# Seven block products for eight: folding 14 units in each of the second and the third feed-forward network, with ten modulation rows moved from the one to the other

## The chip, the cores and the metric

The kernel runs on one core of a Trainium2 chip, as one program. The metric is the device time of one execution in microseconds (us). Engines are named as in the profile: PE is TensorE (matmuls), DVE is VectorE, ACT is ScalarE, SP is SyncE, which here issues the loads.

## The reference

A two-layer transformer with 256 latent tokens (LAT) and 256 context tokens (CTX), width 1024, in fp32. Each layer has a mixer (attention in the first, an mLSTM in the second) between two half feed-forward networks (FFN). The change touches the FFN and the modulation:

```python
def half_ffn(h, shift, scale, gate, w_in, w_out, g, b):
    xm = modulate(h, shift, scale)              # h * (1 + scale) + shift
    a, u = jnp.split(xm @ w_in, 2, axis=-1)     # hidden width D_FF = 2816
    y = (jax.nn.silu(a) * u) @ w_out
    return post_norm(h, 0.5 * gate * y, g, b)   # layer norm of ALPHA * h + delta
```

Shift, scale and gate come from nine 1024-wide modulation vectors per layer, each a 1024 x 1024 block of a matrix times the silu of the conditioning. There is one conditioning vector for LAT and one for CTX.

## The kernel before

**Products.** Activations lie as 8 tiles of 128 features by 512 tokens (LAT in columns 0 to 255, CTX in 256 to 511). Every fp32 value is held as a high and a low fp32r part, so that each product is three matmuls: high-high, high-low and low-high (`mm3`). A loaded fp32 weight chunk of 128x1024 is split in `split`: ScalarE makes the high part (L207), VectorE the low one (L212). Chunks come over the SP queue in program order into raw buffers (4) and are split into pair buffers (7).

**FFN.** There are four, numbered li = 2 * layer + s; "second FFN" is li 1 and "third FFN" is li 2. The hidden width is 22 units of 128. A unit is 48 matmuls with 512 columns (16 products) and gives two PSUM tiles, a and u. ScalarE and VectorE make silu(a) * u from them (L534, L535) and split the result (L212) into the pair `gt[j]`. The units come in parts (11 and 11, or 6, 8 and 8). After the units of a part follow its out products: for each of 8 output tiles d, one product for each unit of the part, and VectorE adds the sum to the residual (L582). The first four units of an FFN (the lead) run on LAT first and then on CTX, with 256 columns, so that they can start while CTX of the stage before is still being normed. In the same way the last d's of the last part (the tail: 4 of them, 6 in the third FFN) run on LAT first and then on CTX. The layer norm of LAT begins inside the LAT tail, after the product that the tables `TAILSTEP` and `FOLDSTEP` name: step m is its sums over features on TensorE (L393), and L486 to L488 write the normed tiles, while TensorE goes on with the rest of LAT and with CTX.

**Folded units.** In the third FFN the units of the second and the third part (16 of 22) are computed with seven block products of half size in place of eight, by Strassen's scheme. A unit is then 84 matmuls of 256 columns (L718) instead of 48 of 512. It needs sums of weight blocks on VectorE (`fold_w`: four sums L689 to L692 of 512 elements, and splits; the first product uses the block "11" that was loaded, the second the sum "s2", which is ready last but one). Sums of activation blocks are made once per FFN (`fold_x`, two calls within the out products of the first part).

**Modulation rows.** A row is one 128x1024 tile of `ada_w`, loaded by `ada_load` (L297) into one of two buffers, and multiplied by the conditioning in `ada_dot` (L303), one dot of 1024 elements on VectorE for each conditioning vector: "both" rows have two dots, single rows one. Rows stand in a list for each FFN and are popped at written-out places: after units ("in"), after out products ("out"). Where a list is used up, a pop does nothing. VectorE carries out its instructions in the program's order, so a dot whose row hasn't landed holds up all that stands behind it.

Of the kernel before, what the change touches and what calls it, by code (L numbers as in the profile page):

```python
# [24 lines left out]
CTX = (256, 512)  # L25
BOTH = (0, 512)
NF = 22
NFH = 11
# [8 lines left out]
RMS_EPS = 1e-6  # L37
HEADS = 8
MH = 4
FOLD = {2: (6, 8, 8)}  # L40
FOLDTAIL = 6
FOLDPOP = {
    2: {
        "lead": (2, 2, 2, 2),
        "in": {4: 3, 5: 3},
        "out": {0: (0, 0, 0, 0, 1, 1, 1, 1), 1: (2, 2, 2, 2, 2, 2, 1, 1)},
    },
}
FOLDX = {0: 0, 2: 1}
# [105 lines left out]
class Body:  # L155
# [382 lines left out]
    def ffn(self, layer, s, gate, groups, side, start=None):  # L538
        nc, V = self.nc, self.nc.vector
        li = layer * 2 + s  # L540
        allg = BOTH
        call = lambda *k: side.get(k, lambda: None)()
        fold = li in FOLD
        parts = FOLD.get(li, (NFH, NFH))
        tail, tailstep = (FOLDTAIL, FOLDSTEP) if fold else (TAIL, TAILSTEP)
        ends = np.cumsum(parts).tolist()
        with self.tc.tile_pool(name=f"ffn{li}", bufs=1) as gp:
# [40 lines left out]
            for hf in range(len(parts)):  # L588
# [12 lines left out]
                        call("in", j)  # L601
                    js = js[LEAD:]
                folded = None
                if fold and hf:
                    self.fine = False
                    folded = self.folded(js, w_in)
                    js = []
# [25 lines left out]
                for d in range(begun, body):  # L633
                    unit_out(hf, d, w, allg)
                    call("out", hf, d)
                    if fold and not hf and d in FOLDX:
                        self.fold_x(2 * FOLDX[d])
                if body < ND:
                    w = Keep(self, w.chunks, SH, w)
                    self.fine = True  # L640
                    for g in groups:
                        for d in range(body, ND):
                            unit_out(hf, d, w, g, tailstep)
                    self.steps(ENDSTEP)


# [783 lines left out]
def emit(ctx, tc, a, out):  # L1430
    b = Body(ctx, tc, a, out)
    nc, V, S = b.nc, b.nc.vector, b.nc.scalar
    b.setup()
    b.setup_rest()
    cpool = b.silu_c()
    both2 = (0, 1)
    queue = [
        [(0, p, both2) for p in range(16, 72)],
        [(1, p, both2) for p in range(40)],
        [(1, p, (0,)) for p in range(40, 72)],  # L1440
    ]
    made = {}

    def once(key, f):
        def get():
            if key not in made:
                made[key] = f()
            return made[key]
        return get

    def side(key, coef, keep=(True, True), nxt=True, ada=(), alone=False, fold=None):
        def pop(n=None):
            for _ in range(n if n is not None else 3 if len(ada) > 40 else 2):
                if ada:
                    b.ada(*ada.pop(0))

        get = once(key, coef)

        b.begin = lambda g: b.norm(g, get, keep[0 if g == LAT else 1], nxt, alone)
        s = {}  # L1460
        if fold:
            for j, n in enumerate(fold["lead"]):
                s["in", j] = lambda n=n: pop(n)
            for j, n in fold["in"].items():
                s["in", j] = lambda n=n: pop(n)
            for hf, ns in fold["out"].items():
                for d, n in enumerate(ns):
                    s["out", hf, d] = lambda n=n: pop(n)
            return s
        for j in range(NF):  # L1470
            s["in", j] = pop
        for d in range(ND):
            s["out", 0, d] = pop
        return s

    both = (LAT, CTX)
    b.ffn(0, 0, once("g0", lambda: b.half_gate(0, 2)), both, side("n0", lambda: b.ln_mod(0, 0, (0, 3)), ada=queue[0]), start)
    assert not queue[0]
    cpool.close()
    b.attention(lambda: b.shift_(0, 5), side("n1", lambda: b.ln_mod(0, 1, (0, 6))))  # L1480
    cpool = b.silu_c()
    b.silu_load()
    b.ffn(0, 1, once("g1", lambda: b.half_gate(0, 8)), both, side("n2", lambda: b.ln_mod(0, 2, (1, 0)), ada=queue[1]))
    assert not queue[1]
    b.ffn(1, 0, once("g2", lambda: b.half_gate(1, 2)), both, side("n3", lambda: b.ln_mod(1, 0, (1, 3)), (True, False), ada=queue[2], fold=FOLDPOP[2]))
    assert not queue[2]
    cpool.close()
    b.mlstm(lambda: b.shift_(1, 5, slice(0, 1)), side("n4", lambda: b.ln_mod(1, 1, (1, 6), 1), alone=True))
    b.ffn_last(1, once("g3", lambda: b.half_gate(1, 8, 1)))
# [5 lines left out]
def _layout(inputs):  # L1495
# [8 lines left out]
    A["ada_w"] = f("ada_w").transpose(0, 2, 1).reshape(2, 72, P, D)  # L1504
    w = f("ffn_w_in").reshape(4, ND, P, 2, NF, P).transpose(0, 4, 2, 1, 3, 5)
    w_in = w.reshape(4, NF, P, 2, 1024).transpose(0, 1, 3, 2, 4).reshape(4, 2 * NF, P, 1024).copy()
    for li, parts in FOLD.items():
        for j in range(parts[0], NF):
            u = w[li, j, :, :, 1, :]
            w_in[li, 2 * j] = w[li, j, :, :, 0, :].reshape(P, 1024)  # L1510
            w_in[li, 2 * j + 1] = np.concatenate([u[:, ND // 2 :], u[:, : ND // 2]], axis=1).reshape(P, 1024)
# [1 line left out]
    A["start_in"] = w[0, :NSTART].transpose(2, 1, 0, 3, 4).reshape(ND, P, 1024)  # L1513
    w = f("ffn_w_out").reshape(4, 2, NFH, P, ND, P).transpose(0, 1, 4, 2, 3, 5)
    w = w.reshape(4, NF * ND, P, P)
    for li, parts in FOLD.items():
        v, at = f("ffn_w_out").reshape(4, NF, P, ND, P)[li].transpose(0, 2, 1, 3), 0
        blocks = []
        for n in parts:
# [69 lines left out]
```

## Time and profile before

| | us |
|---|---|
| median of 3 runs | 1684.46 (1683.39 to 1686.16) |
| the profiled execution, its own time | 1681.06 |
| its span in the trace | 1679.2 |
| mean granted TensorE clock | 0.993 |
| TensorE (PE) busy | 1627.0 (97%) |
| VectorE (DVE) busy | 1328.8 (79%) |
| ScalarE (ACT) busy | 701.3 (42%) |

The profiled execution lies 3.4 us below the median. Times of single places are from the trace, in us from the start of the span. In it the second FFN runs from 578.8 to 948 and the third from 948 to 1304.

### The profile page before, as it was taken

To read this page: it belongs to the slowest core of one execution; us is meant where nothing else is said; L and a number is where in the kernel's file an instruction comes from. 1 tells how busy PE (TensorE), PEld (TensorE's weight loads), DVE (VectorE), ACT (ScalarE), POOL (GpSimd) and SP (SyncE) were. 2 spreads that over 40 slices of the span, in tenths; PEclk is the share of its full clock that TensorE was granted. 3 is DMA by queue.
4 is the path that set the end of the run, shared out by engine and by line. 5 is a ranking of instruction groups with operands and counts; after the bars stand their busy time and mean duration, and the time that the engine had idled before them with its cause. 6 is when DMAs were issued, how large, how long until landed. Compare 5 with 4: busy or idle time off the path is not lost.

```text
span 1679.2 us, 26198 instructions
## 1 busy us (share of the span) xinstructions
PE 1627.0 (97%) x10020; PEld 1454.3 (87%) x10020; DVE 1328.8 (79%) x2864; ACT 701.3 (42%) x1230; POOL 93.4 (6%) x114
## 2 busy tenths in 40 slices
PE   7999999999899999999999999899999999999997
PEld 6888888899888998888888998898999888999986
DVE  6799977749988889996334899887886967997686
ACT  5622222315566362322231452452462656566541
POOL 0000000002321100000000100000001002120000
PEclk9999999999999999999999999999999999999999
DMA  9577766522202337775232254446342332337552
GB/s 355 202 227 232 241 209 194 175 63 86 63 1 68 110 115 226 238 243 170 92 96 89 94 191 144 137 137 193 123 151 76 108 126 76 116 124 250 178 176 74
DMA packets 71918, 250.58 MB, mean 149 GB/s; under 512 B 7921, under 2 KB 10481, under 8 KB 71793
## 3 DMA queue, kind: packets, MB, share of 16 engines
q1 hardware_dynamic: 71072, 248.15, 45.4%
q8 instruction: 78, 1.28, 0.3%
q10 hardware_dynamic: 720, 0.76, 0.1%
q14 instruction: 48, 0.39, 0.1%
HBM read 247.83 MB, written 1.05 MB: 148 GB/s over the span
## 4 chain that ended last, share of the span: by engine, by line
PE 74%; DVE 17%; DMA 4%; ACT 3%; issue 2%; POOL 0%; ACTq 0%; DVEq 0%; SPq 0%; POOLq 0%
PE t L224 19%; PE t L228 19%; PE t L227 19%; DVE t L212 5%; PE t L718 4%; PE t L836 4%; PE t L1333 2%; ACT t L207 2%; DMA t<-in_ada_w 1%; DMA t<-in_ffn_in 1%; PE t L894 1%; PE t L896 1%; PE t L895 1%; PE t L393 1%; DVE t L486 1%
## 5 line engine op out<-in xcount | busy, mean ns | idle before, releaser
L224 PE MATMUL t<-t,t 128*128 128x512 f32 (+2 forms) x2288 | 758.5, 333 | 10.0 <-ACT t L207 6.7
L227 PE MATMUL t<-t,t 128*128 128x256 f32 (+2 forms) x2288 | 759.6, 333 | 1.5 <-DVE t L488 1.2
L228 PE MATMUL t<-t,t 128*128 128x256 f32 (+2 forms) x2288 | 756.2, 332 | 2.5 <-DVE t L212 2.5
L207 ACT CAST t<-t 128x1024 fp32r<-128x1024 f32 (+2 forms) x501 | 426.1, 873 | 534.7 <-PE t L228 231.8
L212 DVE TENSOR_TENSOR t<-t,t 128x256 fp32r<-128x256 f32 (+2 forms) x846 | 528.0, 660 | 137.2 <-ACT t L207 134.7
L224 PEld LDWEIGHTS t<-t,t 128*128 128x128 f32 x2288 | 429.8, 189 | 55.3 <-ACT t L207 9.1
L228 PEld LDWEIGHTS t<-t,t 128*128 128x128 f32 x2288 | 430.5, 188 | 45.9 <-DVE t L212 3.4
L227 PEld LDWEIGHTS t<-t,t 128*128 128x128 f32 x2288 | 431.2, 189 | 45.1 <-DVE t L488 2.1
L303 DVE SCALAR_TENSOR_TENSOR t<-t,t 128x1024 bf16<-128x1024 f32 x224 | 263.0, 1220 | 12.6 <-DMA t<-in_ada_w 12.5
L718 PE MATMUL t<-t,t 128*128 128x256 f32 x1344 | 159.5, 281 | 6.6 <-ACT t L207 4.2
L718 PEld LDWEIGHTS t<-t,t 128*128 128x128 f32 x1344 | 158.0, 191 | 8.4 <-ACT t L207 4.4
L534 ACT ACTIVATE t<-t 128x512 f32<-128x512 f32 (+1 forms) x77 | 37.9, 498 | 148.0 <-PE t L228 147.1
L535 DVE TENSOR_TENSOR t<-t,t 128x512 f32<-128x512 f32 (+1 forms) x77 | 42.9, 562 | 69.4 <-PE t L228 60.8
L430 POOL TENSOR_TENSOR t<-t,t 128x256 f32<-128x256 f32 x30 | 23.3, 777 | 1153.3 <-ACT t L420 1151.8
L582 DVE SCALAR_TENSOR_TENSOR t<-t,t,t 128x256 f32<-128x256 f32 x112 | 50.1, 478 | 40.4 <-PE t L228 40.1
L894 PE MATMUL t<-t,t 128*128 128x256 f32 (+1 forms) x256 | 79.1, 311 | 0.0
L896 PE MATMUL t<-t,t 128*128 128x256 f32 (+1 forms) x256 | 78.6, 309 | 0.0
L895 PE MATMUL t<-t,t 128*128 128x256 f32 (+1 forms) x256 | 78.4, 308 | 0.0
L1333 PE MATMUL t<-t,t 128*128 128x512 f32 (+1 forms) x248 | 55.3, 376 | 10.4 <-ACT t L287 4.9
L1333 PEld LDWEIGHTS t<-t,t 128*128 128x128 f32 x248 | 46.7, 222 | 18.6 <-ACT t L287 4.9
L836 PE MATMUL t<-t,t 128*128 128x512 f32 x264 | 60.0, 389 | 0.0
L836 PEld LDWEIGHTS t<-t,t 128*128 128x128 f32 x264 | 49.5, 188 | 10.2
(185 smaller groups left out, 1250.3 us busy)
## 6 DMA issues: line engine op xcount, KB each, us to landing
t<-in_ffn_in SPq DMA_DIRECT2D x168, 512.0 KB, 4.2
t<-in_ada_w SPq DMA_DIRECT2D x139, 512.0 KB, 4.0
t<-in_ffn_out SPq DMA_DIRECT2D x66, 512.0 KB, 4.2
t<-in_ffn_last SPq DMA_DIRECT2D x22, 512.0 KB, 3.5
t<-in_att_in SPq DMA_DIRECT2D x12, 512.0 KB, 3.5
t<-in_att_out SPq DMA_DIRECT2D x8, 512.0 KB, 3.9
t<-in_ml_qk SPq DMA_DIRECT2D x8, 512.0 KB, 3.4
t<-in_ml_v SPq DMA_DIRECT2D x8, 512.0 KB, 4.4
```

Source lines behind the costliest of these rows:

```text
L207: self.behind(self.nc.scalar.copy(h, x))
L212: self.behind(self.nc.vector.tensor_tensor(out=ls, in0=xs, in1=hs.bitcast(F32), op=ALU.subtract))
L224: ins = mm(out, wh, xh, start=first, stop=False)
L227: mm(out, wh, xl, start=False, stop=False)
L228: mm(out, wl, xh, start=False, stop=last)
L303: ins = nc.vector.scalar_tensor_tensor(self.tmp().bitcast(BF16), r, 1.0, self.cb[:, v, :], ALU.mult, ALU.mult, accum_out=to)
L718: self.pin(nc.tensor.matmul(o, p, q, start=first and k == i == 0, stop=k == half - 1 and i == 2, skip_group_check=True))
L836: pin(nc.tensor.matmul(ys[tt][i], gs[g], ws[k][w][:, i * 512 : (i + 1) * 512], start=k == 0 and g == w == 0, stop=k == NF - 1 and g == 1,))
L894: mm(o, self.xh[:, k, c], wh, start=k == 0, stop=False)
L895: mm(o, self.xh[:, k, c], wl, start=False, stop=False)
L896: mm(o, self.xl[:, k, c], wh, start=False, stop=k == ND - 1)
L1333: mm = lambda *k, **kw: pin(nc.tensor.matmul(*k, **kw))
```

## The change

The second FFN gets three parts of 8, 7 and 7 units instead of 11 and 11, and its last two parts are folded. The third goes from 6, 8 and 8 to 8, 7 and 7. So the number of folded units goes from 0 to 14 in the second and from 16 to 14 in the third. Ten both-rows move from the second FFN's list (40 to 30 rows) to the third's (32 single rows to 10 both and 32 single), and the pops get new tables. The tail of the second FFN has 6 d's instead of 4. Line numbers after the change are 5 or 6 higher than those of before.

```diff
-FOLD = {2: (6, 8, 8)}
+FOLD = {1: ((8, 7, 7), 1), 2: ((8, 7, 7), 1)}
 FOLDTAIL = 6
 FOLDPOP = {
+    1: {
+        "in": {0: 1, 1: 1, 2: 2, 3: 2, 4: 3, 5: 3, 6: 2, 7: 2},
+        "out": {0: (0, 0, 0, 0, 1, 1, 1, 1), 1: (1, 1, 1, 1, 1, 1, 0, 0), 2: (1, 1)},
+        "tail": {(0, 2): 1, (0, 3): 1},
+    },
     2: {
-        "lead": (2, 2, 2, 2),
-        "in": {4: 3, 5: 3},
-        "out": {0: (0, 0, 0, 0, 1, 1, 1, 1), 1: (2, 2, 2, 2, 2, 2, 1, 1)},
+        "in": {0: 3, 1: 3, 2: 3, 3: 3, 4: 5, 5: 5, 6: 4, 7: 4},
+        "out": {0: (0, 0, 0, 0, 1, 1, 1, 1), 1: (2, 2, 2, 2, 2, 2, 0, 0)},
+        "tail": {},
     },
 }
...
-        parts = FOLD.get(li, (NFH, NFH))
+        parts, folds = FOLD.get(li, ((NFH, NFH), 2))
...
-                if fold and hf:
+                if hf >= folds:
                     self.fine = False
                     folded = self.folded(js, w_in)
                     js = []
...
-                    if fold and not hf and d in FOLDX:
+                    if fold and hf == folds - 1 and d in FOLDX:
                         self.fold_x(2 * FOLDX[d])
...
                             unit_out(hf, d, w, g, tailstep)
+                            call("tail", int(g == CTX), d - body)
...
-        [(1, p, both2) for p in range(40)],
-        [(1, p, (0,)) for p in range(40, 72)],
+        [(1, p, both2) for p in range(30)],
+        [(1, p, both2) for p in range(30, 40)] + [(1, p, (0,)) for p in range(40, 72)],
```

The two dots of a both-row stand at three places of the third FFN's order where there were fewer before.

First place: VectorE in the third FFN, the CTX half of the lead, between the product of unit 0 (L535, after the change L540) and that of unit 1. L303 (L308) are dots, L212 (L217) splits of weights. Before:

```order
L535 TENSOR_TENSOR t_9112<-t_9112,t_9063 128x256
L212 TENSOR_TENSOR t_9319<-t_9317,t_9319 128x256
L212 TENSOR_TENSOR t_8801<-t_9112,t_8800 128x256
L303 SCALAR_TENSOR_TENSOR t_9120,t_9117<-t_9118,t_5623 128x1024
L303 SCALAR_TENSOR_TENSOR t_9124,t_9117<-t_9122,t_5623 128x1024
L212 TENSOR_TENSOR t_9319<-t_9317,t_9319 128x256 x3
```

And now:

```order
L217 TENSOR_TENSOR t_9560<-t_9871,t_9559 128x256
L308 SCALAR_TENSOR_TENSOR t_9878,t_7955<-t_9876,t_5623 128x1024
L308 SCALAR_TENSOR_TENSOR t_9880,t_7955<-t_9876,t_5623 128x1024
L308 SCALAR_TENSOR_TENSOR t_9884,t_7955<-t_9882,t_5623 128x1024
L308 SCALAR_TENSOR_TENSOR t_9886,t_7955<-t_9882,t_5623 128x1024
L217 TENSOR_TENSOR t_10115<-t_10113,t_10115 128x256 x3
L217 TENSOR_TENSOR t_10147<-t_10145,t_10147 128x256
L308 SCALAR_TENSOR_TENSOR t_9891,t_9888<-t_9889,t_5623 128x1024
```

Two dots of two rows have become six dots of three rows (the sixth stands behind the piece shown).

Second place: VectorE before the third FFN's out products of the first part. t_9473 is the product of the last plain unit before the change (unit 5), t_10374 and t_10461 are those of units 6 and 7 after it. Before:

```order
L303 SCALAR_TENSOR_TENSOR t_9399,t_9388<-t_9397,t_5623 128x1024
L212 TENSOR_TENSOR t_9752<-t_9750,t_9752 128x256 x2
L535 TENSOR_TENSOR t_9473<-t_9473,t_9406 128x512
L212 TENSOR_TENSOR t_9800<-t_9796,t_9800 128x1024
L212 TENSOR_TENSOR t_9472<-t_9473,t_9471 128x512
```

And now:

```order
L308 SCALAR_TENSOR_TENSOR t_10292,t_10285<-t_10290,t_5623 128x1024
L308 SCALAR_TENSOR_TENSOR t_10296,t_10285<-t_10294,t_5623 128x1024
L308 SCALAR_TENSOR_TENSOR t_10300,t_10285<-t_10298,t_5623 128x1024
L540 TENSOR_TENSOR t_10374<-t_10374,t_10307 128x512
L217 TENSOR_TENSOR t_10373<-t_10374,t_10372 128x512
L308 SCALAR_TENSOR_TENSOR t_10381,t_10285<-t_10379,t_5623 128x1024
L308 SCALAR_TENSOR_TENSOR t_10385,t_10285<-t_10383,t_5623 128x1024
L308 SCALAR_TENSOR_TENSOR t_10389,t_10285<-t_10387,t_5623 128x1024
L308 SCALAR_TENSOR_TENSOR t_10393,t_10285<-t_10391,t_5623 128x1024
L540 TENSOR_TENSOR t_10461<-t_10461,t_10400 128x512
```

The products of units 6 and 7 stand behind five and four dots, each of a row of its own.

Third place: TensorE in those out products after the change (L229, L232, L233 are the three matmuls of `mm3`; t_10372 and t_10373 are the high and low part of `gt[6]`, t_10459 and t_10460 those of `gt[7]`; t_10503 to t_10676 are the PSUM tiles of d 0 to 4):

```order
L229 MATMUL t_10644<-t_10372,t_10647 128x512
L232 MATMUL t_10644<-t_10373,t_10647 128x512
L233 MATMUL t_10644<-t_10372,t_10647 128x512
L229 MATMUL t_10503<-t_10459,t_10506 128x512
L229 MATMUL t_10560<-t_10459,t_10563 128x512
L229 MATMUL t_10592<-t_10459,t_10595 128x512
L232 MATMUL t_10503<-t_10460,t_10506 128x512
L233 MATMUL t_10503<-t_10459,t_10506 128x512
```

The products of the four first d's with units 0 to 6 stand ahead of the first one with unit 7. That is 84 matmuls of the out products, and the first one with unit 6 has 42 of them ahead of it.

Fourth place: VectorE at the end of the third FFN's first out products. L587 (before L582) is the sum of a d, L695 to L698 (L689 to L692) are the sums of weight blocks of the first folded units. Before:

```order
L582 SCALAR_TENSOR_TENSOR t_66<-t_9737,t_9545,t_66 128x256 x2
L690 TENSOR_TENSOR t_9798<-t_9798,t_9796 128x512
L303 SCALAR_TENSOR_TENSOR t_9769,t_9766<-t_9767,t_5623 128x1024
L582 SCALAR_TENSOR_TENSOR t_66<-t_9771,t_9545,t_66 128x256 x2
L303 SCALAR_TENSOR_TENSOR t_9794,t_9766<-t_9792,t_5623 128x1024
L691 TENSOR_TENSOR t_9796<-t_9796,t_9798 128x512
```

And now:

```order
L587 SCALAR_TENSOR_TENSOR t_66<-t_10748,t_10533,t_66 128x256 x2
L217 TENSOR_TENSOR t_10787<-t_10785,t_10787 128x1024
L308 SCALAR_TENSOR_TENSOR t_10782,t_10466<-t_10780,t_5623 128x1024
L217 TENSOR_TENSOR t_10824<-t_10820,t_10824 128x1024
L217 TENSOR_TENSOR t_10827<-t_10822,t_10827 128x512
L695 TENSOR_TENSOR t_10822<-t_10822 128x512
L696 TENSOR_TENSOR t_10822<-t_10822,t_10820 128x512
```

The split of the out products' last weight chunk (t_10787, for d 7) and the splits of the first folded unit's blocks stand here now, behind the sums of d 6. Before the change those splits stood ahead of the sums.

## Rows read from the trace of the kernel before

**Rows 1.** The page's busy times, shares and counts of each engine.

```profile
PE 1627.0 (97%) x10020; PEld 1454.3 (87%) x10020; DVE 1328.8 (79%) x2864; ACT 701.3 (42%) x1230; POOL 93.4 (6%) x114
```

**Rows 2.** Windows, all engines: start:end, length, busy us (instructions), granted clock, DMA share, GB/s.

```profile
628.20:913.80 285.60, 285.60 (x1262) 236.49 (x1261) 191.36 (x309) 76.41 (x91) 0.00 (x0) 1.00 0.53 169
980.70:1057.60 76.90, 72.25 (x392) 62.37 (x391) 68.57 (x143) 25.66 (x38) 0.00 (x0) 0.99 0.56 192
1183.40:1238.20 54.80, 54.70 (x479) 54.51 (x480) 47.03 (x72) 29.88 (x54) 0.00 (x0) 1.00 0.31 97
```

**Rows 3.** Windows of L718 alone (the folded units' matmuls), both blocks.

```profile
1050.50:1134.10 83.60, 78.47 (x648) 77.75 (x648) 0.96 0.43 136
1180.50:1256.40 75.90, 74.31 (x648) 73.72 (x648) 1.00 0.40 125
```

**Rows 4.** Timeline, first folded unit of the third FFN: start, duration, [idle before].

```profile
1050.58 1.58 PE L718 MATMUL t<-t,t 128*128 128x256 f32 x12
1052.15 1.23 DVE L303 SCALAR_TENSOR_TENSOR t<-t,t 128x1024 bf16<-128x1024 f32 x1 [0.50 <-DMA t<-in_ada_w]
1053.91 0.69 DVE L689 TENSOR_TENSOR t<-t 128x512 f32<-128x512 f32 x1
1054.51 0.69 DVE L692 TENSOR_TENSOR t<-t 128x512 f32<-128x512 f32 x1
1056.38 0.79 PE L718 MATMUL t<-t,t 128*128 128x256 f32 x2 [4.22 <-ACT t L207]
1057.64 1.43 PE L718 MATMUL t<-t,t 128*128 128x256 f32 x5 [0.47 <-DVE t L212]
```

**Rows 5.** Windows, all engines, behind that wait (columns as in rows 2).

```profile
1056.40:1063.00 6.60, 6.13 (x27) 5.84 (x28) 4.84 (x5) 2.38 (x4) 0.00 (x0) 0.50 0.52 169
1063.00:1066.00 3.00, 3.00 (x27) 3.00 (x27) 1.83 (x2) 3.00 (x5) 0.00 (x0) 1.00 0.00 1
```

**Rows 6.** VectorE's groups by form: count, busy us, mean ns, idle before.

```profile
L303 DVE SCALAR_TENSOR_TENSOR t<-t,t 128x1024 bf16<-128x1024 f32 x224 | 263.0, 1220 | 12.6 <-DMA t<-in_ada_w 12.5
L212 DVE TENSOR_TENSOR t<-t,t 128x512 fp32r<-128x512 f32 x120 | 81.3, 684 | 11.9 <-ACT t L207 11.6
L582 DVE SCALAR_TENSOR_TENSOR t<-t,t,t 128x256 f32<-128x256 f32 x112 | 50.1, 478 | 40.4 <-PE t L228 40.1
```

**Rows 7.** Timeline of VectorE behind the second FFN's lead.

```profile
632.15 1.22 DVE L303 SCALAR_TENSOR_TENSOR t<-t,t 128x1024 bf16<-128x1024 f32 x1
633.29 0.08 DVE L303 DVE_READ_ACCUMULATOR t<-t,t 128x1 f32 x1
...
635.59 1.22 DVE L212 TENSOR_TENSOR t<-t,t 128x1024 fp32r<-128x1024 f32 x1
637.54 1.23 DVE L303 SCALAR_TENSOR_TENSOR t<-t,t 128x1024 bf16<-128x1024 f32 x1 [0.74 <-DMA t<-in_ada_w]
...
640.16 1.23 DVE L303 SCALAR_TENSOR_TENSOR t<-t,t 128x1024 bf16<-128x1024 f32 x1 [0.24 <-DMA t<-in_ada_w]
```

**Rows 8.** Timeline of VectorE at the third FFN's last lead unit.

```profile
996.81 0.08 DVE L303 DVE_READ_ACCUMULATOR t<-t,t 128x1 f32 x1
...
1003.84 1.23 DVE L303 SCALAR_TENSOR_TENSOR t<-t,t 128x1024 bf16<-128x1024 f32 x1 [1.78 <-DMA t<-in_ada_w]
```

**Rows 9.** Windows of the dots (L303) alone: third FFN, second FFN.

```profile
980.70:1057.60 76.90, 21.84 (x36) 0.99 0.56 192
629.00:742.00 113.00, 70.21 (x120) 1.00 0.74 234
```

**Rows 10.** Timeline, the second FFN's tail and the LAT norm inside it.

```profile
926.70 0.70 PE L393 MATMUL t<-t,t 128*128 128x256 f32 x2
...
948.46 1.28 DVE L488 SCALAR_TENSOR_TENSOR t<-t,t,t 128x256 fp32r<-128x256 f32 x3
...
948.72 0.28 PE L227 MATMUL t<-t,t 128*128 128x256 f32 x1
948.84 0.28 PE L228 MATMUL t<-t,t 128*128 128x256 f32 x1
```

More of the change, by code (lines that the diff above doesn't have):

```diff
@@ L1461, in side @@
         if fold:
-            for j, n in enumerate(fold["lead"]):
-                s["in", j] = lambda n=n: pop(n)
             for j, n in fold["in"].items():
@@ L1468, in side @@
                     s["out", hf, d] = lambda n=n: pop(n)
+            for k, n in fold["tail"].items():
+                s["tail", *k] = lambda n=n: pop(n)
             return s
@@ L1482, in emit @@
     b.silu_load()
-    b.ffn(0, 1, once("g1", lambda: b.half_gate(0, 8)), both, side("n2", lambda: b.ln_mod(0, 2, (1, 0)), ada=queue[1]))
+    b.ffn(0, 1, once("g1", lambda: b.half_gate(0, 8)), both, side("n2", lambda: b.ln_mod(0, 2, (1, 0)), ada=queue[1], fold=FOLDPOP[1]))
     assert not queue[1]
@@ L1506, in _layout @@
     w_in = w.reshape(4, NF, P, 2, 1024).transpose(0, 1, 3, 2, 4).reshape(4, 2 * NF, P, 1024).copy()
-    for li, parts in FOLD.items():
-        for j in range(parts[0], NF):
+    for li, (parts, folds) in FOLD.items():
+        for j in range(sum(parts[:folds]), NF):
             u = w[li, j, :, :, 1, :]
@@ L1515, in _layout @@
     w = w.reshape(4, NF * ND, P, P)
-    for li, parts in FOLD.items():
+    for li, (parts, _) in FOLD.items():
         v, at = f("ffn_w_out").reshape(4, NF, P, ND, P)[li].transpose(0, 2, 1, 3), 0
```

## The prediction

> **What bounds the kernel now.** The page's busy times come first [rows 1]: TensorE is busy for 97% of the span, VectorE for 79%. A saved matmul therefore counts, as long as what feeds TensorE stays in time. As the shares are means over stages, the windows of the stages come next [rows 2]. In the second FFN's plain stretch TensorE has no idle time at all, and VectorE is busy for 191 of 286 us. In the third FFN, from VectorE's first product of the CTX lead (980.7) to the split of "s2" (1057.6), VectorE is busy for 68.6 of 76.9 us: there the two engines are nearly level. Then the windows of the folded matmuls alone [rows 3], and the timeline at the first of them [rows 4]: it is the one place where TensorE waits for VectorE for long.
>
> **Arithmetic: -15.2 us.** In the plain stretch (the first of [rows 2]) 1262 matmuls of 512 columns start in 285.6 us, 226 ns each (227 with two records that are missing). A plain unit is 48 of them: 10.88 us. In a folded stretch (the third of [rows 2]) 479 matmuls of 256 columns take 54.8 us, 114.4 ns each; a folded unit is 84: 9.61 us. The difference is 1.27 us a unit. The second FFN gains 14 folded units, the third loses 2: 12 x 1.27 = 15.2. The out products keep their count; a d in a tail is twice as many matmuls of half the width, which the two rates make equal within 2%.
>
> **The start of folding.** In the third FFN the first block's 648 recorded matmuls lie in 83.6 us [rows 3]; at 114.4 ns they take 74.1. So 9.5 us are lost. The timeline shows the wait [rows 4]: after the twelve matmuls of the first product TensorE is idle for 4.22 us, and again for 0.47, since the sums L689 and L692 stand behind dots and begin only at 1053.9; "s2" is split at 1057.6, where the product before it had ended at 1052.1: 5.5 us late. Behind the wait TensorE's granted clock is 0.50 (its 1.2 GHz level) for 6.6 us and then 1.00 again [rows 5]: some 27 matmuls in 6.1 us where 3.1 would do, about 3 us more. The second block has 75.9 - 74.1 = 1.8 us of loss. The second FFN gets such starts too. There I count VectorE's work over the same stretch in the changed order: 38 dots, 12 splits of 1024, 40 instructions of 512 and 54 of 256, some 100 us by the spacings below, against 104 us of matmuls. It is nearly in time, so I take 4 us for the first start (from 0 to the 9.5 seen) and 1.8 for the second: **+5.8**.
>
> **The third FFN's rows.** VectorE's prices: dots start 1.15 us apart, though each is 1.22 long [rows 6, 7]; in the same way I take 1.14 for a split of 1024, 0.60 for an instruction of 512 and 0.40 for one of 256, each 0.08 under its mean [rows 6]. By the Trainium skill, page "VectorE: DVE Perf Modes", section "The DRAIN you can't avoid", the next instruction doesn't start until the pipe is empty; by full durations the stretch below would come some 12 us longer still (158 instructions by 0.08). The trace disagrees (1.15 apart, 1.22 long), and it decides.
>
> In the stretch from 980.7 to 1057.6 the dots are 18 (the 36 records hold a read of the accumulator for each) [rows 9]. After the change 44 dots stand there: 26 x 1.15 = 29.9 us more. Two plain units more (3.5 each with their splits), two out-weight chunks more (2.3) and 1.8 of the second folded unit's sums, which now stand ahead of "s2", make it 68.6 + 29.9 + 7.0 + 2.3 + 1.8 = 109.6. TensorE's matmuls there are 76.9 - 5.5 = 71.4, plus two plain units (21.8) and 48 more out matmuls (10.9): 104. So VectorE goes from having some slack to being the longer one by 5, even if no row is waited for.
>
> It is worse if the rows come late. There are two buffers, so a row's load can begin only when the dots of the row before the last are done. It lands some 4.25 to 4.6 us after that: a row's dots end at 633.3, those of the next but one begin at 637.5, and again 635.6 and 640.2, both waiting for the load [rows 7]. In the busiest place seen it was 7.0 (996.8 to 1003.8) [rows 8]. A pair of both-rows then takes 4.4 + 2.3 = 6.7 us, and a pair of single rows 4.4 + 1.15 = 5.55. Up to the last unit of the first part there are now 10 both-rows (33.5 us) and 20 single ones (55.5): 89 us, where the lead and the four plain units last only about 59 on TensorE. By that chain, the product of unit 6 comes at about 75 us from the stretch's start and that of unit 7 at 87. TensorE reaches the first use of them at 59 + 42 x 0.227 = 68.5 and 59 + 84 x 0.227 = 78. Behind the last of these rows (94, with the wait for the first) VectorE still has 24 instructions of the activations' sums (14.4), nine sums of a d (3.6), four dots (4.6), two splits of 1024 (2.3), one of a half chunk in two (1.2), six weight sums (3.6), the split "s2" (1.1) and a wait for the raw weights (1.3): "s2" at about 126, where TensorE could be there at 104. That is 22 us late in place of 5.5, **+17**; some of it is cover for other waits, and the clock's loss stands in both, so I take **+15**. Its bounds: with no row waited for, "s2" is ready at 109.6, as late as before, +0. With 4.8 us to land, 28 late, +22; with the 7.0 of [rows 8] throughout, about +30. I choose the middle because the second FFN's 60 dots take 113 us for 30 rows [rows 9], 3.8 us a row, a little slower even than a both-row's 3.35. What the second FFN gives up is no gain, since TensorE never waited there [rows 2].
>
> **The tails: +3.5.** In the second FFN's tail the sums of the LAT norm (m) begin at 926.7, and the last normed tile is written at 949.7 [rows 10], 23.0 us later. 155 of the tail's 264 matmuls, 0.12 us apart, and some 2 us of the norm's own cover it, to about 948; the next lead reaches the last tile 42 matmuls (5 us) after that, at 953, so there were about 3.3 us of slack. In the new order only 113 of 252 stand behind m: 42 x 0.12 = 5.0 less cover, a wait of 1.7, and I take 2. The third FFN has 137 behind m for 158: 2.5 less, for which I take 1.5. Bounds 0 (cover elsewhere) and 7.5 (no slack at all).
>
> **Sum.** -15.2 + 5.8 + 15 + 3.5 = +9.1 against the profiled execution's 1681.1: 1690.2. The median of the runs is 3.4 above that execution, so the forecast for the median is 1693.6, rounded to **1694**.
>
> **Rivals.**
>
> *The gain comes through (faster).* The rows land in time, because plain units leave the loads of weights room, and the third FFN's first folded unit starts no later than before. For it: single loads have been as fast as 4.25, and VectorE's count is only 5 us over TensorE's. Against it: the chain of two buffers. Then -15.2 + 5.8 + 0 + 3.5 = -5.9, and with no cost in the tails or at the second FFN's first start -13.4: 1671 to 1679 on the median. It decides if the last plain unit's product comes before 78 us of the stretch. By the Trainium skill, page "Perfetto Trace Analysis", section "Identifying the Most-Contended Engine", the most occupied engine is the one to relieve, which here is TensorE; by that alone the whole 15.2 would come through, 1669. The trace agrees on the shares [rows 1], not on this stretch [rows 2].
>
> *Even.* The row chain costs half of what I take (7 to 10 us): what the second FFN gains the third gives up. 1683 to 1688.
>
> *Saturated.* Rows take the 7.0 us of [rows 8], as weights for two more units, chunks of the out weights and rows all load there at once: +30 in place of +15, 1708.
>
> *The change does nothing* is excluded: the order has 2352 folded matmuls for 1344.
>
> **How the numbers follow.** The forecast case (+4 to +18 over before, 1688 to 1702) has a chance of 0.47, saturated 0.09, even 0.17, and the gain 0.27. 0.2% is 3.4 us, about what a measurement of this kernel can tell from no change: under 1681.1 is faster, over 1687.8 slower. So faster 0.27, same 0.17, slower 0.56. The range must leave out no more than 2 in 10: from 1675, which holds over half of the gain case, to 1706, which leaves out most of the saturated one. The forecast case's own range is 1688 to 1702.
>
> **What would show it.** The second FFN's folded blocks run at 114 to 118 ns a matmul, with under 4 us of idle time at the first "s2"; the stage from lead to tail is some 12 us shorter. In the third FFN, VectorE shows waits for `ada_w` of 1 to 3 us at most rows from the CTX lead on, TensorE waits in the first out products before `gt[6]` and `gt[7]`, and the lower clock follows each. If VectorE is busy without gaps there, the rows were in time and the cost is 0 to 5 us. Wrong would be: no wait of TensorE between the lead and the first L724; or a wait in the second FFN as long as the third's, for which the order gives no reason; or a tail in which TensorE stands still for more than 4 us.

## The result and the profile after

The changed kernel takes 1692.1 us (median of 6 runs, 1689.7 to 1693.9), where the kernel before takes 1684.5 (median of 6 runs, 1682.7 to 1686.2). The measured ratio is 1.0035, with a 95% interval of 1.0024 to 1.0047: slower, by about 6 us; the two medians given here lie 7.6 us apart. The profiled execution took 1693.94 us with a span of 1692.1. It is the slowest of its six, 1.8 us above their median, and that of before lies 3.4 us below its own median, so the two traces are 12.9 us apart.

The page's busy times answer to [rows 1]:

```profile
PE 1624.0 (96%) x10428; PEld 1468.1 (87%) x10428; DVE 1410.3 (83%) x2993; ACT 739.8 (44%) x1312; POOL 94.7 (6%) x114
```

TensorE's busy time is 3 us less than before and the span 13 longer, so TensorE is idle for 16 us more than before: the time is lost in waits. VectorE's share has risen by four points. The next table cuts both traces at the first matmul of each stage, which the timeline gives; for each it has the length in us. Matmuls that moved between the out products and a tail explain 1.4 us of the second FFN's rows and 4.1 of the third's.

| stage | before | changed |
|---|---|---|
| second FFN: lead | 49.4 | 51.7 |
| second FFN: units, out products | 285.6 | 275.2 |
| second FFN's tail and the third's lead | 82.3 | 83.6 |
| third FFN: plain units, first out products | 54.4 | 106.4 |
| third FFN: first folded block | 83.5 | 68.8 |
| third FFN: from there to the tail | 136.1 | 119.1 |
| from the third FFN's tail to the end | 409.0 | 408.2 |

The third FFN's plain stage has 96 + 48 matmuls of 512 columns more than before, which take 32.7 us, and became 52 longer. Windows over all engines, as in [rows 2]: the plain stage of the second FFN, then the stretch of the third that the prediction counted, from VectorE's first product of the CTX lead to TensorE's start on "s2":

```profile
630.70:717.80 87.10, 87.10 (x387) 72.13 (x386) 83.27 (x146) 24.94 (x34) 0.00 (x0) 1.00 0.57 177
974.26:1099.86 125.60, 109.70 (x535) 92.32 (x533) 110.14 (x204) 36.84 (x55) 0.00 (x0) 0.93 0.62 208
```

In the second FFN TensorE is busy without a gap, though VectorE is busy for 83 of 87 us. In the third, VectorE is busy for 110.1 of 125.6 us and TensorE for 109.7: neither is full. VectorE waits for rows (10.1 us), for ScalarE's high parts (4.3) and hardly for TensorE (0.8), and TensorE waits for what VectorE makes. The timeline of TensorE's waits over 0.7 us in that stretch, from the plain units on ([idle before <- what ended it]):

```profile
1048.11 1.65 PE L229 MATMUL t<-t,t 128*128 128x512 f32 x3 [5.33 <-ACT t L212]
1088.35 0.80 PE L233 MATMUL t<-t,t 128*128 128x512 f32 x1 [8.78 <-DVE t L217]
1098.55 0.51 PE L724 MATMUL t<-t,t 128*128 128x256 f32 x2 [0.98 <-ACT t L735]
1099.86 0.38 PE L724 MATMUL t<-t,t 128*128 128x256 f32 x1 [0.81 <-DVE t L217]
```

The first wait is for `gt[6]`, the second for the low part of the last out-weight chunk, the third for ScalarE's copy of a folded product (L735) and the last for "s2". The single wait of 4.2 us at "s2" before [rows 4] has become two longer ones ahead of it. Windows around them (all engines, granted clock third from the end) show the lower clock after each, as in [rows 5]:

```profile
1048.00:1053.00 5.00, 4.89 (x12) 3.88 (x13) 3.06 (x5) 0.56 (x2) 0.00 (x0) 0.52 0.94 352
1053.00:1060.00 7.00, 7.00 (x33) 5.79 (x32) 4.43 (x7) 0.62 (x1) 0.00 (x0) 1.00 0.73 208
1088.00:1092.00 4.00, 3.65 (x9) 2.89 (x10) 3.93 (x7) 0.00 (x0) 0.00 (x0) 0.50 0.87 262
```

What VectorE waits for ahead of the first of them is seen in its timeline, and summed in its groups by form from the last lead unit to "s2" (count, busy us, mean ns, idle before):

```profile
1040.70 1.22 DVE L308 SCALAR_TENSOR_TENSOR t<-t,t 128x1024 bf16<-128x1024 f32 x1 [1.67 <-DMA t<-in_ada_w]
1042.91 1.22 DVE L308 SCALAR_TENSOR_TENSOR t<-t,t 128x1024 bf16<-128x1024 f32 x1 [0.98 <-DMA t<-in_ada_w]
1045.58 1.23 DVE L308 SCALAR_TENSOR_TENSOR t<-t,t 128x1024 bf16<-128x1024 f32 x1 [1.43 <-DMA t<-in_ada_w]
```

```profile
L308 DVE SCALAR_TENSOR_TENSOR t<-t,t 128x1024 bf16<-128x1024 f32 x37 | 44.6, 1220 | 10.2 <-DMA t<-in_ada_w 10.1
```

Row after row is waited for here, and the product of unit 6 stands behind them. In the whole stretch 11 of the 30 rows are waited for; six of them, at the last plain units, make 7.8 of the 10.1 us. The windows of the folded matmuls, as [rows 3] (564 in a block of seven units): the second FFN's two blocks and the third's first.

```profile
717.78:785.60 67.82, 65.32 (x564) 64.45 (x563) 1.00 0.43 137
826.70:893.40 66.70, 66.20 (x563) 65.80 (x563) 1.00 0.40 125
1096.00:1164.60 68.60, 66.30 (x563) 65.68 (x563) 0.98 0.41 131
```

At 114.4 ns each, 564 are 64.5 us: up to the first matmul behind them the blocks take 67.9, 66.9 and 68.8 us, so they lose 3.4, 2.3 and 4.2.

The tail of the second FFN answers to [rows 10]. From the timeline, the sums m, the last normed tiles of LAT and a matmul of the third FFN's lead that waits for the norm; then the window of all engines from the tail's start to the end of that lead, after and before:

```profile
922.57 0.62 PE L398 MATMUL t<-t,t 128*128 128x256 f32 x2
...
939.59 0.85 PE L229 MATMUL t<-t,t 128*128 128x256 f32 x5 [0.59 <-ACT t L492]
...
944.30 1.26 DVE L493 SCALAR_TENSOR_TENSOR t<-t,t,t 128x256 fp32r<-128x256 f32 x3
```

```profile
905.90:989.50 83.60, 81.06 (x667) 78.91 (x667) 80.64 (x215) 36.33 (x74) 7.89 (x10) 1.00 0.36 113
913.82:996.15 82.33, 80.90 (x679) 79.78 (x678) 68.58 (x192) 37.40 (x78) 8.04 (x10) 1.00 0.32 111
```

### The profile page after: what moved, and what is told of

Its sections match the earlier page's. It is cut to its first block, busy times and chain, and to the rows that moved or that the text cites. A ratio compares the mean times of both kernels' runs of the same rounds, so it can differ in the third digit from the quotient of the medians.

```text
span 1692.1 us, 27210 instructions
## 1 busy us (share of the span) xinstructions
PE 1624.0 (96%) x10428; PEld 1468.1 (87%) x10428; DVE 1410.3 (83%) x2993; ACT 739.8 (44%) x1312; POOL 94.7 (6%) x114
## 4 chain that ended last, share of the span: by engine, by line
PE 69%; DVE 20%; DMA 5%; ACT 4%; issue 2%; POOL 0%; ACTq 0%; DVEq 0%; SPq 0%; POOLq 0%
PE t L229 16%; PE t L233 15%; PE t L232 15%; PE t L724 10%; DVE t L217 6%; PE t L842 4%; ACT t L212 2%; DVE t L308 2%; DMA t<-in_ffn_in 2%; PE t L1339 2%; DMA t<-in_ada_w 1%; PE t L901 1%; PE t L900 1%; PE t L902 1%; PE t L398 1%
## 5 line engine op out<-in xcount | busy, mean ns | idle before, releaser
L229 PE MATMUL t<-t,t 128*128 128x256 f32 (+2 forms) x2088 | 683.6, 331 | 17.5 <-ACT t L212 12.3
L212 ACT CAST t<-t 128x1024 fp32r<-128x1024 f32 (+2 forms) x533 | 451.8, 869 | 554.9 <-PE t L233 164.3
L233 PE MATMUL t<-t,t 128*128 128x256 f32 (+2 forms) x2088 | 682.9, 329 | 12.0 <-DVE t L217 12.0
L232 PE MATMUL t<-t,t 128*128 128x256 f32 (+2 forms) x2088 | 686.4, 330 | 2.2 <-DVE t L493 1.4
L217 DVE TENSOR_TENSOR t<-t,t 128x256 fp32r<-128x256 f32 (+2 forms) x869 | 556.5, 675 | 108.6 <-ACT t L212 97.3
L229 PEld LDWEIGHTS t<-t,t 128*128 128x128 f32 x2088 | 393.5, 190 | 57.4 <-ACT t L212 14.9
L233 PEld LDWEIGHTS t<-t,t 128*128 128x128 f32 x2088 | 395.2, 190 | 50.0 <-DVE t L217 14.0
L232 PEld LDWEIGHTS t<-t,t 128*128 128x128 f32 x2088 | 396.0, 190 | 39.7 <-DVE t L493 3.0
L724 PE MATMUL t<-t,t 128*128 128x256 f32 x2352 | 276.0, 279 | 6.5 <-ACT t L744 2.9
L308 DVE SCALAR_TENSOR_TENSOR t<-t,t 128x1024 bf16<-128x1024 f32 x224 | 264.0, 1219 | 17.9 <-DMA t<-in_ada_w 17.5
L587 DVE SCALAR_TENSOR_TENSOR t<-t,t,t 128x256 f32<-128x256 f32 x128 | 57.2, 477 | 26.7 <-PE t L233 26.4
L539 ACT ACTIVATE t<-t 128x256 f32<-128x256 f32 (+1 forms) x65 | 30.7, 480 | 100.1 <-PE t L233 98.9
L540 DVE TENSOR_TENSOR t<-t,t 128x256 f32<-128x256 f32 (+1 forms) x65 | 34.5, 539 | 31.5 <-PE t L233 27.1
```

The source lines that it names most:

```text
L212: self.behind(self.nc.scalar.copy(h, x))
L217: self.behind(self.nc.vector.tensor_tensor(out=ls, in0=xs, in1=hs.bitcast(F32), op=ALU.subtract))
L229: ins = mm(out, wh, xh, start=first, stop=False)
L232: mm(out, wh, xl, start=False, stop=False)
L233: mm(out, wl, xh, start=False, stop=last)
L308: ins = nc.vector.scalar_tensor_tensor(self.tmp().bitcast(BF16), r, 1.0, self.cb[:, v, :], ALU.mult, ALU.mult, accum_out=to)
```

## The experiments

Theory A is that of the prediction: the third FFN's rows land late since a row's load must wait for the dots two rows before, and these waits hold up VectorE and then TensorE. Theory B: VectorE simply has too much work there. Theory C: the rate of the loads is the limit. Each kernel was run beside the kernel before on the same chip, and ratios are to that.

### Four buffers for the rows of the plain units

```diff
+NROW = 4
...
-        r = self.t([P, 1024], tag="ada", bufs=2, pool=self.gp)
+        if layer == 1 and 30 <= dt < 60:
...
+            r = self.t([P, 1024], tag="ada3", bufs=NROW, pool=self.rp)
+        else:
+            r = self.t([P, 1024], tag="ada", bufs=2, pool=self.gp)
```

The memory for them is that of the activations' sums, which are made only later. The order of VectorE's instructions isn't quite that of the changed kernel.

> The changed kernel with four buffers instead of two for the thirty rows that the third FFN pops in its plain units. Theory A (rows land late because a load must wait for the dots two rows before): VectorE's waits for ada_w, some 10 us before the first out products, go, the waits of TensorE before gt[6] (5.3 us) and before the last out-weight chunk (8.8 us) mostly go with them, and the time falls by 10 to 14 us, to about 1680. Theory B (VectorE has too much work there, whatever the loads do): the time falls by 3 us at most. Theory C (the loads' rate is the limit, since rows and weights are loaded at once): the waits for ada_w stay, and weights come later than before; 1688 to 1695.

It took 1680.0 us, 0.9958 of before (0.9945 to 0.9971): 12 us less than the changed kernel, from slower to faster than before. The dots by form, from the CTX lead on, and the window of the third FFN's plain stage, both of this kernel:

```profile
L316 DVE SCALAR_TENSOR_TENSOR t<-t,t 128x1024 bf16<-128x1024 f32 x43 | 50.2, 1218 | 0.1
```

```profile
991.00:1087.30 96.30, 90.06 (x387) 72.91 (x386) 93.41 (x169) 29.27 (x41) 0.00 (x0) 0.98 0.65 221
```

The waits for rows are gone (0.1 us for 10.1), and the stage is 96.3 us for 106.4. That is theory A. Theories B and C fall as main causes: the dots (44 up to "s2") and the loads are those of the changed kernel, and at 221 GB/s every row lands in time. But VectorE is now busy for 93.4 of 96.3 us, and TensorE still waits for it (3.6 and 2.4 us): behind the row waits, its work is the next bound.

### Rows that stay in place

```diff
+        if layer == 1 and dt >= 30:
+            if dt == 30:
+                self.rows = []
+            if len(self.rows) == 2:
+                return self.rows[dt % 2]
         r = self.t([P, 1024], tag="ada", bufs=2, pool=self.gp)
         self.nc.sync.dma_start(r, self.a["ada_w"][layer, dt])
+        if layer == 1 and dt >= 30:
+            self.rows.append(r)
```

> The changed kernel with only two of the third FFN's rows loaded; all its dots are done on these two, so VectorE has the same work, and forty row loads are left out (the modulation of the second layer is then another one). Theory A and theory C: no dot waits, the losses of the third FFN's start fall to those of before, 1677 to 1680. Theory B: within 3 us of the changed kernel, 1689 to 1693.

This kernel leaves out forty row loads, so it computes another modulation and is of use as a measurement only. It took 1676.2 us, 0.9941 of before (0.9929 to 0.9953), just under the 1677 to 1680 of theories A and C. The third FFN's plain stage in it:

```profile
989.30:1081.90 92.60, 88.23 (x386) 71.79 (x385) 92.04 (x163) 28.71 (x39) 0.00 (x0) 1.00 0.27 88
```

VectorE is busy for 92.0 of 92.6 us, and the stage is 5.5 longer than the 87.1 that its matmuls take in the second FFN. So that is what VectorE's work costs by itself in this order, close to the prediction's "longer by 5".

### Rows spread later

```diff
-        "in": {0: 3, 1: 3, 2: 3, 3: 3, 4: 5, 5: 5, 6: 4, 7: 4},
-        "out": {0: (0, 0, 0, 0, 1, 1, 1, 1), 1: (2, 2, 2, 2, 2, 2, 0, 0)},
-        "tail": {},
+        "in": {0: 2, 1: 2, 2: 2, 3: 2, 4: 3, 5: 3, 6: 2, 7: 2},
+        "out": {0: (0, 0, 0, 0, 1, 1, 1, 1), 1: (2, 2, 2, 2, 2, 2, 2, 2), 2: (1, 1)},
+        "tail": {(0, 2): 1, (0, 3): 1},
```

> The changed kernel with the third FFN's pops spread over all of it: 18 rows in the plain units instead of 30, then 4, 16, 2 and 2 in the tail. Theory A: up to the first folded unit the chain of ten both-rows and eight single ones takes 56 us and is no longer than TensorE's work, and s2 is ready before TensorE asks for it: the 23.6 us lost between the first plain unit and the end of the first folded block fall to 3 to 6, the time by 17 to 20 us, less 0 to 5 that the rows cost in the second out products: 1672 to 1678. Theory B: twelve dots fewer are 13.8 us: 1678 to 1680. If the loss has to do with the division in parts of 8, 7 and 7 and not with the rows: 1688 or more.

It took 1678.6 us, 0.9954 (0.9942 to 0.9966). That is just above theory A's 1672 to 1678 and inside theory B's 1678 to 1680, so the total doesn't tell them apart. The stages do: the plain stage takes 87.1 us and the first block 65.6, for 106.4 and 68.8, which is 22.5 us less, where A gave 17 to 20 and B 13.8. But the second block loses 11.5 us more than in the changed kernel, where 0 to 5 were expected. TensorE's wait in it, and the cast on ScalarE just ahead of the copy (L738) that ends it:

```profile
1195.21 2.08 PE L724 MATMUL t<-t,t 128*128 128x256 f32 x8 [7.30 <-ACT t L738]
1194.68 0.21 ACT L212 CAST t<-t 128x16 fp32r<-128x16 f32 x1 [4.36 <-DVE t L409]
```

The sixteen dots are popped in the second out products (41 us), and some of them run into the block. ScalarE's cast is of small values made from the modulation, which VectorE copies (L409) only at 1194.4; the weight sums ahead of it had been done at 1187.3, and three more dots and three splits stand in between. So TensorE waits mostly for VectorE's work behind the sums. The block takes 77.2 us for 65.7. So the next kernel takes some of the rows back.

```diff
-        "in": {0: 2, 1: 2, 2: 2, 3: 2, 4: 3, 5: 3, 6: 2, 7: 2},
-        "out": {0: (0, 0, 0, 0, 1, 1, 1, 1), 1: (2, 2, 2, 2, 2, 2, 2, 2), 2: (1, 1)},
+        "in": {0: 2, 1: 2, 2: 2, 3: 2, 4: 4, 5: 4, 6: 3, 7: 3},
+        "out": {0: (0, 0, 0, 0, 1, 1, 1, 1), 1: (2, 2, 2, 2, 1, 1, 1, 1), 2: (1, 1)},
```

> The changed kernel with the third FFN's pops spread out: 22 in the plain units, 4, 12, 2 in the three out products and 2 in the tail (18, 4, 16, 2, 2 in the kernel with late rows, whose second block began with a wait of 7.4 us). Theory A: the chain before the first block takes 67 us, and the product of the last plain unit comes ahead of TensorE's need; the second out products have 12 rows, 33 us for 41: no wait of more than 2 us at either block. 1670 to 1675, 3 to 8 us faster than with late rows. If rows in the out products delay the sums in any case: 1678 or more.

With 22 rows in the plain units and 12 in the second out products it took 1673.7 us, 0.9924 (0.9912 to 0.9936), within the range expected. The third FFN's plain stage, and the dots up to the first block:

```profile
990.00:1079.40 89.40, 87.99 (x386) 71.96 (x386) 84.18 (x153) 28.96 (x39) 0.00 (x0) 1.00 0.63 217
```

```profile
L308 DVE SCALAR_TENSOR_TENSOR t<-t,t 128x1024 bf16<-128x1024 f32 x28 | 33.5, 1218 | 3.9 <-DMA t<-in_ada_w 3.8
```

Some rows are still waited for (3.8 us), but VectorE now has the slack for it: the plain stage loses 2.4 us in place of 19.4.

### Single rows first

```diff
-        [(1, p, both2) for p in range(30, 40)] + [(1, p, (0,)) for p in range(40, 72)],
+        [(1, p, (0,)) for p in range(40, 72)] + [(1, p, both2) for p in range(30, 40)],
```

> The changed kernel with the third FFN's list in another order: first the 32 single rows, then the ten both-rows (all of them done before the tail). Thirty single rows stand in the plain units. Theory A (two buffers, 4.4 us to land and 1.15 for each dot): the chain is 30 x 2.78 = 83 us in place of 89, s2 is some 6 us earlier, still late: 5 to 7 us faster than the changed kernel, TensorE's wait before gt[6] about 4 us shorter. Theory B (VectorE's work): ten dots fewer before s2, 11.5 us, so 10 to 13 us faster. If the ten both-rows are the whole cause: as in the kernel with four buffers.

It took 1695.0 us, 1.0047 (1.0033 to 1.0061), no faster than the changed kernel: a miss for every theory as written. TensorE's wait before `gt[6]` is 4.0 us for 5.3, not 4 shorter. The dots from the plain units to "s2", and TensorE at "s2":

```profile
L308 DVE SCALAR_TENSOR_TENSOR t<-t,t 128x1024 bf16<-128x1024 f32 x31 | 37.7, 1222 | 17.5 <-DMA t<-in_ada_w 17.4
```

```profile
1093.41 0.80 PE L724 MATMUL t<-t,t 128*128 128x256 f32 x2 [9.06 <-ACT t L212]
```

There are fewer dots than in the changed kernel and more waits for rows, 17.4 us for 10.1: what a dot less saves, the load takes back. That speaks for A against B. TensorE is done waiting for "s2" 106.5 us after the start of the plain stage, for 110.3: 3.8 us earlier where A gave 6. What A's expectation left out is that both-rows now fall into the out products: the second folded block takes 69.1 us for 65.7 and gives most of it back. That the ten both-rows by themselves are the cause is ruled out: thirty single rows in the same places do as much.

### The tail

Two kernels change the second FFN's tail only. In the first it has 4 d's again (`TAIL` and `TAILSTEP` for the second FFN), in the second its two rows are popped in the second out products:

```diff
-        "out": {0: (0, 0, 0, 0, 1, 1, 1, 1), 1: (1, 1, 1, 1, 1, 1, 0, 0), 2: (1, 1)},
-        "tail": {(0, 2): 1, (0, 3): 1},
+        "out": {0: (0, 0, 0, 0, 1, 1, 1, 1), 1: (1, 1, 1, 1, 1, 1, 1, 1), 2: (1, 1)},
+        "tail": {},
```

> The changed kernel with a tail of 4 d's in place of 6 in the second FFN (the third's stays). In the new order 95 matmuls of the tail stand behind the norm's sums m, for 113 in the changed kernel and 155 before it. Cover theory: 18 x 0.12 = 2.2 us less cover, so the third FFN's lead ends about 2 us later: 1.5 to 3 us slower than the changed kernel. If the length of the tail has no part in its loss: within 1 us of the changed kernel.

> The changed kernel with the two rows that the second FFN pops in its tail popped in its second out products instead. In the order m moves from the 139th to the 115th of the tail's 252 matmuls, so 137 stand behind it. Cover theory: 24 x 0.12 = 2.9 us more cover, and the tail's loss of 2 to 3 us goes: the stage from the second FFN's tail to the end of the third's lead is 2 to 3 us shorter, the kernel 2 to 3 us faster. If the loss of the tail comes from its six d's with twice as many narrow matmuls: no change.

With 4 d's it took 1694.6 us, 1.0050 (1.0037 to 1.0063). The stages from the last out products to the end of the next lead take 100.0 us for 96.0, more than the 1.5 to 3 expected, in the direction of the cover theory; inside the norm TensorE now waits 3.8 us in one place. Without tail rows the time is 1692.4, 1.0034 (1.0022 to 1.0045), not to be told from the changed kernel. The stage itself, however, as above:

```profile
905.70:987.30 81.60, 80.80 (x668) 79.28 (x667) 77.73 (x210) 37.73 (x77) 8.59 (x10) 1.00 0.33 104
```

It is 2.0 us shorter with the same matmuls, as expected; that the whole kernel would be 2 to 3 us faster did not come true. So most of the tail's loss goes with its two rows (four dots) and not with the number of d's. The edit does two things: m comes 24 matmuls earlier, and VectorE has four dots (4.6 us) less to do in a stage where it is nearly full. The run doesn't part them. The same edit on top of the spread rows:

> The kernel with spread rows, and besides the second FFN's two tail rows popped in its second out products (as in the kernel without tail rows, where the stage from the tail to the end of the next lead was 2.0 us shorter). If that adds up: 1671 to 1673, the stage from tail to end of lead 81 to 82 us for 83.7. If the 2 us are given back at the second block, as the total of the kernel without tail rows suggests: 1673 to 1675.

1672.5 us, 0.9911 (0.9895 to 0.9927): the stage takes 81.4 us for 83.7, but the second FFN's second block 67.1 for 65.5, so most of it is given back. The two expectations meet at 1673, and the time does not tell them apart. By its median it is the fastest kernel of this study, some 14 us faster than before on the same chip; the interval overlaps that of the spread rows alone.

### Only the second FFN

```diff
-FOLD = {1: ((8, 7, 7), 1), 2: ((8, 7, 7), 1)}
+FOLD = {1: ((8, 7, 7), 1), 2: ((6, 8, 8), 1)}
```

The third FFN and its rows are as before the change. All forty rows are popped in the second: 18, 4, 12, 4, and 2 in the tail.

> Only the second FFN folded, all forty rows kept in it (two or three a unit, two an out product, two in the tail), the third FFN and its 32 single rows as in the kernel before. By the stages of the changed kernel, the second FFN's start of lead to the third's end of lead was 6.8 us shorter, so 1676 to 1679, up to 3 more if the ten rows make its first folded unit late. If the second FFN's folding costs what it saves and the third is not to blame: 1684 or more.

It took 1704.2 us, 1.0109 (1.0093 to 1.0125): 25 us over the 1676 to 1679 that the stages gave, and in the range of the other case, "1684 or more". The timeline of TensorE at the second FFN's second block:

```profile
842.68 0.80 PE L724 MATMUL t<-t,t 128*128 128x256 f32 x2 [11.51 <-ACT t L212]
```

Twelve both-rows in 41 us of out products, 24 dots, delay the block's weight sums; it takes 80.3 us for 66.8. The first block takes 70.5 for 67.9, and the stage with the tail, which gets two more rows ahead of it, 92.2 for 83.6. So with these places a folded second FFN has no room for forty both-rows. That moving ten of them away costs something is no reason that leaving them costs less. No other places for them were tried. That the third FFN is not to blame in the changed kernel, as the other case has it, doesn't follow: its 13.6 us of loss are measured there.

### The third FFN in its old parts

```diff
-FOLD = {1: ((8, 7, 7), 1), 2: ((8, 7, 7), 1)}
+FOLD = {1: ((8, 7, 7), 1), 2: ((6, 8, 8), 1)}
```

Here the row lists are those of the changed kernel, with the third FFN's rows spread.

> Second FFN and row lists as in the changed kernel, the third FFN in its old parts of 6, 8 and 8 with the 42 rows spread over it (16 in the plain units, 6, 14, 4, and 2 in the tail). Theory A with VectorE's work: up to s2 there are 32 dots for 18 before, 16 us more on a VectorE that was already 5.5 us late, so s2 is 13 us late or more, and the last plain unit's product comes after about 56 us where TensorE can use it from 37 on: the third FFN's start loses 10 to 15 us more than with spread rows in parts of 8, 7 and 7; two more folded units give 2.5 back: 1681 to 1688. If the parts of 8, 7 and 7 in the third FFN do nothing for the rows: 1670 to 1673.

It took 1688.6 us, 1.0012 (1.0002 to 1.0022), 15 more than with parts of 8, 7 and 7 and spread rows, just over the 1681 to 1688 that were expected. TensorE in the first out products:

```profile
1046.19 0.80 PE L233 MATMUL t<-t,t 128*128 128x512 f32 x1 [11.46 <-DVE t L217]
```

The plain stage and the first block lose 18.3 us here, for 3.9 with spread rows. So the two more plain units, at a cost of 2.5 us, are what gives VectorE the time for the ten rows; the places of the rows differ a little as well (16 in the plain units for 22).

## Why the prediction was right

The median came out at 1692.1 for 1694, and its main step is shown: with two buffers the third FFN's rows come late, they hold up VectorE and then TensorE, and with four buffers the kernel is 12 us faster. Some other terms came out near their numbers for reasons that are not those given, which is luck.

**Arithmetic, -15.2.** It came through: the folded blocks run at 114.4 ns a matmul plus losses, and the plain ones at 227. (The 1262 records of [rows 2] are the 1260 matmuls of the stretch and two that reach into it; none are missing.)

**The start of folding in the second FFN, +5.8.** Measured 3.4 + 2.3 = 5.7, but not by the step that was named. At neither start does TensorE wait for weight sums on VectorE, as it did in [rows 4]. Its waits over 0.3 us in the two blocks are ended by ScalarE's copies of folded products (L735, L744): 0.45, 0.41 and 1.64 us in the first, the longest far behind the start, and 0.45 in the second. That VectorE would be nearly in time was right (its count adds up to 103 us rather than some 100); that the number agrees is luck.

**The third FFN's rows, +15.** Measured +13.6: the plain stage loses 19.4 us (106.4 against 87.1 for its 384 matmuls), the first block 4.2 and the second 1.2, together 24.8, where before it was 9.4 + 1.8 = 11.2. The stretch from VectorE's first product to "s2" is 125.6 us where 126 was worked out, with 110.1 of work where 109.6 was counted. The products of units 6 and 7 began 72.5 and 83.0 us into it, for 75 and 87. The split of the total was off, though, and its closeness is in part luck: the rows were waited for 10.1 us and not some 15, since at the first nineteen rows VectorE's other work mostly covered the landing (2.3 us of waits); another 5 us were waits for ScalarE's high parts and for TensorE, for which 1.3 was set. So the sign "waits at most rows from the CTX lead on" came at 11 of 30 rows, with 0.2 to 1.7 us. TensorE waited before `gt[6]` only, not before `gt[7]`, since the first wait covered the second; the longest wait was at the last out-weight chunk, which the changed order puts behind the activations' sums. The prediction had it in the sum, but not among the signs. The upper bound "about +30" for 7.0 us throughout doesn't follow from the prediction's own chain: fifteen pairs at 2.6 us more are 39 us, which added to +17 makes about +55. The four buffers and the resident rows show the cause: without row waits the loss of the three places falls from 24.8 us to 11.6 (plain stage 9.2, blocks 1.0 and 1.4) with four buffers, about what it was before the change, and to 7.3 (5.5, 0.9, 0.9) with resident rows. What remains there goes with a VectorE that is busy nearly all the time.

**The tails, +3.5.** Measured 2.7 for the second FFN: 83.6 us for 82.3, with 12 narrow matmuls (1.4 us) fewer. Cover is a part of it: with m at its new place TensorE waits 0.59 us for the norm's tiles, where a wait of 1.7 was worked out. The other waits over 0.3 us there are in the third FFN's lead, 0.75 us for the split of a weight chunk on VectorE and 0.53 for ScalarE. For them the prediction had no term: VectorE is busy for 80.6 of 83.6 us in this stage, for 68.6 of 82.3 before. All three are gone in the kernel without tail rows, so most of the loss was avoidable. That two rows popped in the tail put m later, and load VectorE there, the prediction did not say. From the third FFN's tail to the end it was 3.4 for 1.5: 408.2 us where 36 matmuls fewer would make 404.8 of 409.0. In the kernel without tail rows, whose program from there on is the same, it was 408.8, and with four buffers 406.2, so a part of it is the spread between executions. Together the tails cost 6.1 us for 3.5.

**The rest.** The lead of the second FFN, which the change doesn't touch, took 2.3 us more in this trace, at a granted clock of 0.74 for 0.87 in the 13 us from 577 on. In the traces of the ten experiments it took 49.7 to 50.9, at 0.87, so this trace stands out. The terms give -15.2 + 5.7 + 13.6 + 2.7 + 3.4 + 2.3 = 12.5 of the 12.9 us between the traces, 3.4 more than the sum of 9.1 that was forecast. By the medians the kernel lost 7.6, 1.5 less than that. Which of the terms are smaller in the other executions is not shown.

**The rivals.** The gain that comes through is what the kernel with spread rows shows, at 1673.7, within the 1671 to 1679 worked out: its point of decision, the last plain unit's product ahead of TensorE's need, is what those edits changed. By the Trainium skill, page "Perfetto Trace Analysis", section "Identifying the Most-Contended Engine", the engine with the highest occupancy is to be optimised first; the estimate from that alone, with all of the 15.2 us saved, was 1669. The changed kernel doesn't agree with this estimate, with 1692.1. The kernel with spread rows and none in the second FFN's tail, at 1672.5, comes near it. The even rival and the saturated one did not come. The even one gave 1683 to 1688, and the row chain cost 13.6 us for its 7 to 10. For the saturated one, the single rows that VectorE waited for in a row began 2.2 to 2.7 us apart, near the 2.8 of the forecast's chain, where 7.0 us to land and one dot for each pair need 4.1 for each row.

## What to carry to other kernels

Where two engines are nearly level in a stage, count the second engine's work stage by stage, and spread small jobs until no stage's count exceeds its cover: work that is free in one stage is not free in the next. With two buffers a pair of jobs takes a landing time and the work on one of them; if that is more than the stage gives, more buffers (12 us here) or fewer jobs there (18 us) help, while cheaper jobs mostly lengthened the wait. Before a change is written off as slower, see whether its loss lies in the change or in where its companions stand: here the same folding is 0.35% slower or 0.8 to 0.9% faster than before, by the places of some ten rows.

## What the runs showed of the hardware

Less work on VectorE did not mean an earlier row: with the single rows first it had fewer dots and waited 17.4 us for loads where the changed kernel waited 10.1. Not explained is that the plain stage with rows that stay in place is 3.7 us shorter than with four buffers, though in both no row is waited for; the order of VectorE's instructions differs between the two, and the runs don't say whether that or the loads' traffic (88 against 221 GB/s) has a part in it.
